# A third load buffer for the tap matrices, one ring for projection inputs and GLU outputs, and another order of the convolution stage

## The chip, the cores and the metric

The kernel runs on one core of one Trainium2 chip. The metric is the device time of one execution in microseconds, as the median of several. A core has TensorE (PE: matrix multiplication, its sums in PSUM banks), VectorE (DVE) and ScalarE (ACT) for work on elements, GpSimd (POOL), which here also issues some transfers, and SyncE (SP), which issues most of them. Each engine takes its instructions in a fixed order and waits for semaphores of the others. Data move between DRAM and the on-chip memory (SBUF, 128 partitions) by DMA engines.

## The reference, cut to what matters

One step of a decoder trunk on 512 prompt tokens and 8 × 8 sample tokens, of width 1024. The stage that is changed is the convolution module of the first layer; the per-layer input `p` of both layers enters far later, but its projection is computed here.

```python
def _conv_module(xn, hist, w_pw1, b_pw1, w_dw, b_dw, ln_g, ln_b, w_pw2, b_pw2):
    u = xn @ w_pw1 + b_pw1
    a, g = jnp.split(u, 2, axis=-1)
    u = a * jax.nn.sigmoid(g)
    ...
    uh = jnp.concatenate([hist.astype(u.dtype), u], axis=1)
    c = _dwconv_valid(uh, w_dw) + b_dw          # 31 taps, each channel by itself
    c = jax.nn.silu(_layernorm(c, ln_g, ln_b))
    return c @ w_pw2 + b_pw2, uh[:, -(CONV_K - 1):]

def _ple(h, p, g, w_gate, w_proj):
    gate = jax.nn.sigmoid(_rmsnorm(h, g) @ w_gate)
    return h + gate * (p @ w_proj)
```

## The kernel before

Each fp32 product is made of three products of rounded parts. A matrix is split into a high part (a cast on ACT, line 172) and a low part (original minus high, on DVE, line 175; for some weights on POOL). TensorE multiplies high by high (184), high by low (186) and low by high (187).

The convolution stage runs from about 50 to 345 us. Tokens are in two parts: part 0 has 256 of the prompt, part 1 the other 256 and the 64 of the samples (320). The 1024 channels are eight blocks m of 128. What happens to a block:

- `pw1(m, part)` (the letter a of the order table): two products into PSUM, `pg` and `pa`, 24 matmuls each; then sigmoid and gate give `u`, a tile in a ring of UB = 3 buffers with the tag "u".
- `d`: `u` is written to DRAM (`d_u`). `regroup(m)` (m in the table) reads it back in another layout into `x`, with 32 channels and 4 pieces of time across the partitions, and splits it into `xx`.
- `taps(m, g)` (c), g = 0 to 3: the prompt's convolution for 32 channels, as 9 pairs of matmuls with a tap matrix. In each pair line 609 multiplies both parts of `xx` by the high part `th`, and line 610 the high part of `xx` by the low part `tl`. There are 32 of these matrices; c(7,3) is the last. `taps_dma(i)` loads matrix i from DRAM into `traw`, on POOL's queue, in a ring of TR = 2 buffers; `taps_load(i)` casts and subtracts it into `th` and `tl`, rings of TB = 2, and then asks for the load of matrix i + TR. Where c(m,g) stands in the table, the split of the next matrix is asked for too. The sums `cps` go out of PSUM as `v` by ACT (613) and DVE (614).
- `ungroup(m)` (b): `v` is written to DRAM (`d_c`, four transfers) and, after that, read back in the first layout into `h` (two transfers), all on SyncE's queue.
- `taps_smp` (o, O): the samples' taps, a product on POOL (636), its sums on DVE.
- `ln_stat(m)` (s): DVE subtracts a mean estimate from block m of `h` (710), ACT squares it (`lsq`, 714), DVE adds the squares up (716), and TensorE forms column sums `lns` (725).

When all eight blocks are in, `ln_y` (L) turns `lns` into factors with a chain of small DVE instructions, and TensorE spreads these over the partitions (`R`). `ln_apply(part)` (M) normalizes and gives `hn`, which the second product `p` (w) takes.

Between these the projection of the per-layer input runs, which depends on none of them: `proj_in(l, part)` (i) loads the input of layer l, `proj_split` (j) splits it into two tiles `pT` with a ring of 4 buffers of their own, and `proj(l, part, half)` (p in the table) is 24 matmuls into four PSUM banks named `proj`. They are copied into `pst` by ACT or DVE (496), a ring of two buffers, and every second copy is followed by a write to DRAM (`d_pp`). All in all there are 192 of these matmuls, 32 copies and 16 writes. `ucat`, in which POOL gathers the last rows of `u` for an output, also has the tag "pst".

The order of each engine's instructions is set by a scheduler from priorities. The priorities follow the order in which the code is emitted, which in this stage is the table `CONV`: one token per step, a letter and its indices, as in

```
a6,0 c3,0 s0 c3,1 o4 j0,0 a6,1 d6 c3,2 O4 c3,3 b3 m5
```

Of the kernel before, what the change touches and what calls it, by code (L numbers as in the profile page):

```python
# [9 lines left out]
F32 = mybir.dt.float32  # L10
F32R = mybir.dt.float32r
# [6 lines left out]
P = 128  # L18
D = 1024
KD = D // P  # L20
# [3 lines left out]
CK = 31  # L24
TAPS = 36
TB = 2
TR = 2
UB = 3
QSB = 5
LBUF = 4  # L30
CONV = """
X0 a0,0 X1 a1,0 a2,0 a0,1 d0 a1,1 d1 o0 m0 a2,1 d2 O0
a3,0 c0,0 m1 c0,1 o1 a3,1 d3 c0,2 O1 c0,3 b0 m2
a4,0 c1,0 c1,1 o2 a4,1 d4 c1,2 O2 c1,3 b1 m3
a5,0 c2,0 k c2,1 o3 a5,1 d5 c2,2 O3 c2,3 b2 m4
a6,0 c3,0 s0 c3,1 o4 j0,0 a6,1 d6 c3,2 O4 c3,3 b3 m5
a7,0 c4,0 s1 c4,1 o5 i0,0 j0,1 c4,2 O5 c4,3 b4 m6 s2
p0,0,0 c5,0 c5,1 o6 i0,1 j1,0 a7,1 d7 c5,2 O6 c5,3 b5 m7 s3
p0,0,1 c6,0 i1,0 j1,1 c6,1 o7 P p0,1,0 c6,2 O7 c6,3 b6 s4
p0,1,1 c7,0 i1,1 c7,1 p1,0,0 c7,2 c7,3 b7 s5  # L40
p1,0,1 s6 s7 L p1,1,0 M0 p1,1,1
w0,0 w1,0 M1 w0,1 w2,0 w1,1 w3,0 n0 w2,1 r0 w3,1 n1 r1
"""
SCHED = """
# [120 lines left out]
class Trunk:  # L165
# [309 lines left out]

    def proj_split(self, l, part, sp):
        n, raw = PN[part], self.praw.pop((l, part))
        pT = [sp.tile([P, 640], F32R, tag="pT", name="pT", bufs=4)[:, :2 * n].rearrange("p (k t) -> p k t", k=2) for _ in range(2)]
        self.hi(pT[0], raw)
        self.lo(pT[1], raw, pT[0])  # L480
        self.pT[l, part] = pT
# [21 lines left out]
    def conv_stage(self):  # L503
# [15 lines left out]
        with tc.tile_pool(name="w2c", bufs=2) as w2, tc.tile_pool(name="cvp", bufs=2) as sp:  # L519
# [13 lines left out]
            def pw1(m, part):  # L533

                n = PN[part]
                if part == 0:
                    us[m] = sp.tile([P, 816], F32, tag="u", name="u", bufs=UB)
                    keep(nc.sync.dma_start(out=us[m][:, 512:], in_=a["sc"][m]))
# [15 lines left out]
                    self.done(("pw1", m, 0), ("pw1", m, 1))  # L554
                    self.V.scalar_tensor_tensor(out=smp(u, 30, 8), in0=pa[:, 256:320].rearrange("p (b t) -> p b t", b=8), scalar=ba, in1=sg[:, 256:320].rearrange("p (b t) -> p b t", b=8), op0=ALU.add, op1=ALU.mult)

            ucat = sp.tile([P, KD, 96], F32, tag="pst", name="ucat")

            def u_out(i):
                keep(nc.gpsimd.tensor_copy(out=ucat[:, i, 0:32].rearrange("p (r q) -> p r q", r=4), in_=us[i][:, 0:512].rearrange("p (r q) -> p r q", r=4)[:, :, 120:128]))  # L560
# [18 lines left out]
            def taps_dma(i):  # L579
                if i < 4 * KD and i not in traw and i not in tw:  # L580
                    traw[i] = sp.tile([P, 32 * TAPS], F32, tag="traw", name="traw", bufs=TR)
                    keep(nc.gpsimd.dma_start(out=traw[i], in_=a["tw"][i]))

            def taps_load(i):
                if i >= 4 * KD or i in tw:
                    return
                taps_dma(i)
                h, l = (sp.tile([P, 32 * TAPS], F32R, tag=n, name=n, bufs=TB) for n in ("th", "tl"))
                raw = traw.pop(i)
                self.hi(h, raw)  # L590
                self.lo(l, raw, h)
                tw[i] = h, l
                taps_dma(i + TR)

            vs = {}

# [19 lines left out]
            def ungroup(m):  # L616

                v = vs.pop(m)
                for r in range(4):
                    nc.sync.dma_start(out=d_c[m][:, :, r].rearrange("g c j -> c g j"), in_=v[32 * r:32 * r + 32])  # L620
                dv = d_c[m].rearrange("g c r j -> (g c) r j")
                for part in PARTS:
                    nc.sync.dma_start(out=cc[part][:, m, 0:256].rearrange("p (r j) -> p r j", r=4), in_=dv[:, :, part * 64:part * 64 + 64])
# [26 lines left out]
            for e in CONV.split():  # L650
                kind, v = e[0], [int(d) for d in e[1:].split(",") if d]
# [14 lines left out]
                    taps(*v)  # L666
                elif kind == "b":
                    ungroup(*v)
                elif kind == "P":
                    dm = self.smp.tile([P, 1], F32, tag="rs_t", name="dm")  # L670
                    self.after(self.A.activation(out=dm, in_=self.zero[:, 0:1], func=AF.Silu), self.sig)
# [714 lines left out]
```

## Time and profile before

| | us |
|---|---|
| median of three runs | 1532.9 |
| lowest and highest of them | 1531.63, 1534.46 |
| the profiled execution | 1532.51 |
| its span | 1530.7 |
| TensorE busy in the span | 1463.4 (96%) |
| VectorE, ScalarE, GpSimd busy | 1041.9, 724.8, 286.6 |
| TensorE busy, 50 to 345 us | 255.60 of 295.00 |
| issue to landing of a tap matrix (576 KB) | 5.1 |

The span is what lies between the first and the last instruction of the profiled execution; its own time has 1.8 us more. The granted clock of TensorE has two levels, shown as 1.00 (2.4 GHz) and 0.50 (1.2 GHz). In a timeline a row is a run of like instructions: start, busy time, engine, line, operation, tiles, count, and in brackets how long the engine was idle before it and what ended this. A row of a wait view gives the waiting engine, tile and line, the releaser, and then total, count and longest.

### The profile page before, as it was taken

What the parts mean: (1) busy time and instruction counts of PE and PEld (TensorE: products, weight loads), DVE (VectorE), ACT (ScalarE), POOL (GpSimd) and SP (SyncE); (2) the same over time, 40 slices, a digit from 0 to 9 for tenths busy, and PEclk for the clock granted to TensorE, in tenths of its full rate; (3) what the DMA queues carried; (4) which work ended last, traced back from release to release, by engine and by line L of the source; (5) the groups of instructions that cost most, each with busy time, mean ns of one, the idle gap of its engine ahead of it and who ended that gap; (6) DMA issues with size and microseconds to landing.
All of it is one profiled execution on the core that took longest, in us unless ns stands there. A gap on an engine that the chain in (4) does not pass through costs nothing.

```text
span 1530.7 us, 27978 instructions
## 1 busy us (share of the span) xinstructions
PE 1463.4 (96%) x10807; PEld 1439.1 (94%) x10807; DVE 1041.9 (68%) x2352; ACT 724.8 (47%) x1580; POOL 286.6 (19%) x430
## 2 busy tenths in 40 slices
PE   8999886899999999999999997999999999999998
PEld 8899776899999999999999996798999999999998
DVE  7687683768655665656877899948765656564774
ACT  5444352635443444444645667744543525252641
POOL 1244440021111211111001333322211111011100
PEclk9999997999999999999999999999999999999999
DMA  5666564433228232323233222214231313131412
GB/s 211 203 203 181 179 215 135 126 122 102 77 76 186 76 103 64 104 66 100 87 115 127 84 70 71 76 52 133 84 97 56 104 49 119 48 122 45 147 46 73
DMA packets 68805, 165.83 MB, mean 108 GB/s; under 512 B 15216, under 2 KB 31056, under 8 KB 68624
## 3 DMA queue, kind: packets, MB, share of 16 engines
q1 hardware_dynamic: 61728, 134.96, 28.7%
q0 software_dynamic: 6640, 28.46, 6.3%
q8 instruction: 85, 1.39, 0.4%
q10 hardware_dynamic: 304, 0.62, 0.1%
q14 instruction: 48, 0.39, 0.1%
HBM read 151.13 MB, written 18.72 MB: 111 GB/s over the span
## 4 chain that ended last, share of the span: by engine, by line
PE 75%; DVE 6%; ACT 2%; issue 1%; DMA 0%; SPq 0%; DVEq 0%; ACTq 0%
PE up L186 12%; PE up L187 12%; PE up L184 12%; PE dn L187 6%; PE dn L186 6%; PE dn L184 6%; PE plg L187 2%; PE plg L186 2%; PE plg L184 2%; PE p L186 1%; PE wo L187 1%; PE wo L184 1%; PE wo L186 1%; PE p L187 1%; PE p L184 1%; DVE qs L175 1%
## 5 line engine op out<-in xcount | busy, mean ns | idle before, releaser
L186 PE MATMUL up<-hn,wh 128*128 128x256 f32 (+1 forms) x1408 | 415.3, 297 | 3.3 <-DVE hn L175 3.3
L187 PE MATMUL up<-hn,wl 128*128 128x256 f32 (+1 forms) x1408 | 413.9, 296 | 0.9 <-DVE wl L175 0.9
L184 PE MATMUL up<-hn,wh 128*128 128x256 f32 (+1 forms) x1408 | 409.8, 296 | 1.0 <-ACT hn L172 1.0
L172 ACT CAST wh<-raw 128x1024 fp32r<-128x1024 f32 x196 | 203.1, 1047 | 307.9 <-PE up L186 173.9
L175 DVE TENSOR_TENSOR wl<-raw,wh 128x1024 fp32r<-128x1024 f32 x173 | 224.0, 1302 | 159.1 <-ACT wh L172 157.3
L186 PEld LDWEIGHTS up<-hn,wh 128*128 128x128 f32 x1408 | 266.1, 189 | 4.1 <-DVE hn L175 3.9
L187 PEld LDWEIGHTS up<-hn,wl 128*128 128x128 f32 x1408 | 266.0, 189 | 1.2 <-DVE wl L175 1.1
L184 PEld LDWEIGHTS up<-hn,wh 128*128 128x128 f32 x1408 | 264.6, 190 | 1.4 <-ACT hn L172 1.4
L187 PE MATMUL dn<-fh,wl 128*128 128x320 f32 (+1 forms) x704 | 208.6, 296 | 0.0
L184 PE MATMUL dn<-fh,wh 128*128 128x320 f32 (+1 forms) x704 | 207.8, 295 | 0.0
L186 PE MATMUL dn<-fl,wh 128*128 128x320 f32 (+1 forms) x704 | 207.7, 295 | 0.0
L797 POOL COPY stash<-ue 128x18 f32<-128x18 f32 x88 | 71.4, 813 | 540.0 <-ACT ue L794 538.4
L827 DVE TENSOR_TENSOR h<-dn,h 128x256 f32<-128x256 f32 (+1 forms) x192 | 87.4, 456 | 98.1 <-PE dn L187 97.9
L184 PEld LDWEIGHTS dn<-fh,wh 128*128 128x128 f32 x704 | 133.6, 190 | 0.0
L187 PEld LDWEIGHTS dn<-fh,wl 128*128 128x128 f32 x704 | 133.0, 189 | 0.0
L186 PEld LDWEIGHTS dn<-fl,wh 128*128 128x128 f32 x704 | 132.9, 189 | 0.0
L609 PE MATMUL cps<-xx,th 128*128 128x256 f32 x288 | 73.8, 343 | 19.1 <-ACT th L172 14.9
L233 POOL TENSOR_TENSOR wl<-raw,wh 128x1024 fp32r<-128x1024 f32 x23 | 55.5, 2425 | 141.8 <-ACT wh L172 130.5
L609 PEld LDWEIGHTS cps<-xx,th 128*128 128x128 f32 x288 | 56.5, 196 | 21.0 <-ACT th L172 16.7
L187 PE MATMUL plg<-hn,wl 128*128 128x256 f32 (+1 forms) x256 | 76.1, 297 | 0.0
L186 PE MATMUL plg<-hn,wh 128*128 128x256 f32 (+1 forms) x256 | 75.9, 297 | 0.0
L184 PE MATMUL plg<-hn,wh 128*128 128x256 f32 (+1 forms) x256 | 75.9, 296 | 0.0
(255 smaller groups left out, 3301.7 us busy)
## 6 DMA issues: line engine op xcount, KB each, us to landing
raw<-in_w_dram SPq DMA_DIRECT2D x196, 512.0 KB, 3.7
traw<-in_tw_dram POOLq DMA_DIRECT2D x32, 576.0 KB, 5.1
bias<-d_bias SPq DMA_DIRECT2D x8, 512.0 KB, 4.5
d_bias<-d_ext POOLq DMA_DIRECT2D x1, 3064.0 KB, 24.8
h<-in_x_dram SPq DMA_DIRECT2D x4, 640.0 KB, 5.4
d_pp<-pst SPq DMA_DIRECT2D x8, 320.0 KB, 3.3
pp<-d_pp SPq DMA_DIRECT2D x8, 320.0 KB, 3.3
d_u<-u SPq DMA_DIRECT2D x8, 256.0 KB, 4.2
```

The lines of the kernel that those rows point to most:

```text
L172: return self.A.copy(out=out, in_=in_)
L175: self.V.tensor_tensor(out=out, in0=in_, in1=hi.bitcast(F32), op=ALU.subtract)
L184: self.after(mm(out, lhsT=wh, rhs=xh, start=start, stop=False), self.hold)
L186: mm(out, lhsT=wh, rhs=xl, start=False, stop=False)
L187: mm(out, lhsT=wl, rhs=xh, start=False, stop=stop)
L233: nc.gpsimd.tensor_tensor(out=l, in0=raw, in1=h.bitcast(F32), op=ALU.subtract)
L609: self.T.matmul(ps[:, 0:2 * P], lhsT=h[:, w], rhs=z[:, :, g, d:d + P], start=d == 0, stop=False)
L797: nc.gpsimd.tensor_copy(out=self.stash[:, :, :, blk], in_=tail)
L827: self.V.tensor_tensor(out=self.h[part][:, m], in0=ps[:, :n], in1=self.h[part][:, m], op=ALU.add)
```

## The change

- The ring of `traw` has three buffers instead of two (TR), and `taps_load(i)` asks for the loads i + 1 to i + TR in order, instead of only i + TR.
- The ring "u" has four buffers instead of three (UB), and `pT` takes its tiles from it. `ucat` has a buffer of its own.
- The transfers `h` of `ungroup` become a step of their own, `bring(m)` (the letter e), which the table has one row later.
- The table is reordered. Before, 144 of the 192 projection matmuls run before the last tap is done and 48 behind `lns`; now 66 run before the last tap is done, 30 between it and `lns`, and 96 behind `lns`. The loads and splits of the projection's inputs (i, j) follow.

```diff
-TR = 2
-UB = 3
+TR = 3
+UB = 4
 ...
-a6,0 c3,0 s0 c3,1 o4 j0,0 a6,1 d6 c3,2 O4 c3,3 b3 m5
+a6,0 c3,0 e2 s0 c3,1 o4 a6,1 d6 c3,2 O4 c3,3 b3 m5
 ...
-p1,0,1 s6 s7 L p1,1,0 M0 p1,1,1
+p0,1,0 p0,1,1 i1,1 s6 s7 L p1,0,0 p1,0,1 M0 p1,1,0 p1,1,1
 ...
-        pT = [sp.tile([P, 640], F32R, tag="pT", name="pT", bufs=4)[:, :2 * n].rearrange("p (k t) -> p k t", k=2) for _ in range(2)]
+        pT = [sp.tile([P, 816], F32R, tag="u", name="pT", bufs=UB)[:, :2 * n].rearrange("p (k t) -> p k t", k=2) for _ in range(2)]
 ...
-            ucat = sp.tile([P, KD, 96], F32, tag="pst", name="ucat")
+            ucat = sp.tile([P, KD, 96], F32, tag="ucat", name="ucat", bufs=1)
 ...
                 tw[i] = h, l
-                taps_dma(i + TR)
+                for k in range(1, TR + 1):
+                    taps_dma(i + k)
 ...
                     nc.sync.dma_start(out=d_c[m][:, :, r].rearrange("g c j -> c g j"), in_=v[32 * r:32 * r + 32])
+
+            def bring(m):
                 dv = d_c[m].rearrange("g c r j -> (g c) r j")
                 for part in PARTS:
                     nc.sync.dma_start(out=cc[part][:, m, 0:256].rearrange("p (r j) -> p r j", r=4), in_=dv[:, :, part * 64:part * 64 + 64])
 ...
+                elif kind == "e":
+                    bring(*v)
```

The first taps. POOL's transfers before (a number tells one tile from another of its name; `DMASW` and `DVE` in brackets are the semaphores that an issue waits for):

```order
L582 DMA traw_795<-in_tw_dram 128x1152
L582 DMA traw_801<-in_tw_dram 128x1152
L582 DMA traw_803<-in_tw_dram 128x1152 [waits DMASW0_49,DVE_49]
L582 DMA traw_809<-in_tw_dram 128x1152 [waits DMASW2_49,DVE_49]
L582 DMA traw_844<-in_tw_dram 128x1152 [waits DMASW1_49,DVE_49]
```

and now:

```order
L582 DMA traw_795<-in_tw_dram 128x1152
L582 DMA traw_801<-in_tw_dram 128x1152
L582 DMA traw_803<-in_tw_dram 128x1152
L582 DMA traw_805<-in_tw_dram 128x1152 [waits DMASW0_49,DVE_49]
L582 DMA traw_811<-in_tw_dram 128x1152 [waits DMASW1_49,DVE_49]
```

The third load no longer waits for a buffer. ACT at the same place, before, where th_805 is the second tap matrix and th_840 the third:

```order
L172 CAST th_797<-traw_795 128x1152 [waits DMASW0_49]
L172 CAST xx_646<-x_171 128x544 [waits DMAHW5_49,DMAHW4_49,DMAHW6_49,DMAHW3_49,Pool_49]
L172 CAST wh_736<-raw_734 128x1024 [waits DMAHW0_49,PE_49]
L548 ACTIVATE sg_790<-sg_790,cols_116 128x256 [waits DVE_49,Activation_49]
L613 ACTIVATE v_830<-cps_811,cols_116 128x128 [waits PE_49]
L172 CAST th_805<-traw_803 128x1152 [waits DMASW2_49]
L172 CAST th_840<-traw_801 128x1152 [waits DMASW1_49,Activation_49]
```

and now, with th_807 the second and th_842 the third:

```order
L172 CAST th_797<-traw_795 128x1152 [waits DMASW0_49]
L172 CAST xx_646<-x_171 128x544 [waits DMAHW5_49,DMAHW4_49,DMAHW6_49,DMAHW3_49,Pool_49]
L172 CAST wh_736<-raw_734 128x1024 [waits DMAHW0_49,PE_49]
L172 CAST th_807<-traw_801 128x1152 [waits DMASW1_49]
L548 ACTIVATE sg_790<-sg_790,cols_116 128x256 [waits DVE_49,Activation_49]
L172 CAST th_842<-traw_803 128x1152 [waits DMASW2_49,PE_49,Activation_49]
L614 ACTIVATE v_832<-cps_813,cols_116 128x128 [waits PE_49]
```

The second matrix is now the one that is loaded second, and its cast has moved ahead of the gate `sg`.

The last taps. ACT before, from the cast of matrix (7,2) to that of (7,3), with `lsq` of block 6 between them:

```order
L172 CAST th_2587<-traw_2477 128x1152
L714 ACTIVATE lsq_2762<-h0_91 128x256
L714 ACTIVATE lsq_2768<-h1_92 128x320
L613 ACTIVATE v_2580<-cps_2591,cols_116 128x128
L496 COPY pst_2631<-proj_2633 128x256
L613 ACTIVATE v_2580<-cps_2664,cols_116 128x128
L496 COPY pst_2649<-proj_2642 128x256
L496 COPY pst_2649<-proj_2651 128x256
L172 CAST th_2660<-traw_2559 128x1152
```

and now, where th_2503 is (7,2) and th_2530 is (7,3):

```order
L496 COPY pst_2460<-proj_2453 128x256
L496 COPY pst_2460<-proj_2462 128x256
L172 CAST th_2503<-traw_2359 128x1152
L614 ACTIVATE v_2494<-cps_2475,cols_116 128x128
L647 ACTIVATE h1_92<-pc_2384,cols_116 128x64
L614 ACTIVATE v_2494<-cps_2507,cols_116 128x128
L172 CAST th_2530<-traw_2395 128x1152
L614 ACTIVATE v_2494<-cps_2534,cols_116 128x128
L719 ACTIVATE lsq_2678<-h0_91 128x256
```

The square of block 6 has moved behind the last cast, and the copies into `pst` that stood ahead of that cast are gone. DVE there, before (tl_2661 is the low part of (7,3), and h0_91 with lnk in the last row is the subtraction of block 7):

```order
L716 TENSOR_TENSOR lss_1635<-lss_1635,lsq_2768 128x320
L614 TENSOR_TENSOR v_2580<-cps_2591,v_2580 128x128
L496 COPY pst_2631<-proj_2612 128x256
L614 TENSOR_TENSOR v_2580<-cps_2664,v_2580 128x128
L175 TENSOR_TENSOR tl_2661<-traw_2559,th_2660 128x1152
L496 COPY pst_2732<-proj_2734 128x256
L614 TENSOR_TENSOR v_2580<-cps_2685,v_2580 128x128
L710 TENSOR_TENSOR h0_91<-h0_91,lnk_1363 128x256
```

and now (tl_2504 is that of (7,2), tl_2531 that of (7,3), h0_91 with lnk is the subtraction of block 6):

```order
L175 TENSOR_TENSOR tl_2504<-traw_2359,th_2503 128x1152
L615 TENSOR_TENSOR v_2494<-cps_2475,v_2494 128x128
L615 TENSOR_TENSOR v_2494<-cps_2507,v_2494 128x128
L715 TENSOR_TENSOR h0_91<-h0_91,lnk_1365 128x256
L175 TENSOR_TENSOR tl_2531<-traw_2395,th_2530 128x1152
L715 TENSOR_TENSOR h1_92<-h1_92,lnk_1369 128x320
L615 TENSOR_TENSOR v_2494<-cps_2534,v_2494 128x128
```

The subtraction of block 6, which stood further ahead, is now between the last two low parts.

The end. TensorE before, from the last two matmuls of c(7,3):

```order
L609 MATMUL cps<-xx,th 128x256
L610 MATMUL cps<-xx,tl 128x128
L725 MATMUL lns<-ones,h_91 128x1 x2
L725 MATMUL lns<-ones,h_92 128x1 x3
L725 MATMUL lns<-ones,h_91 128x1 x2
L725 MATMUL lns<-ones,h_92 128x1 x3
L725 MATMUL lns<-ones,h_91 128x1 x2
L725 MATMUL lns<-ones,h_92 128x1 x3
L725 MATMUL lns<-ones,lss 128x1 x5
L184 MATMUL proj<-pT,wh 128x320
L186 MATMUL proj<-pT,wh 128x320
```

and now, from the last two of the thirty `proj` matmuls that follow c(7,3):

```order
L186 MATMUL proj<-pT,wh 128x320
L187 MATMUL proj<-pT,wl 128x320
L730 MATMUL lns<-ones,h_91 128x1 x2
L730 MATMUL lns<-ones,h_92 128x1 x3
L730 MATMUL lns<-ones,h_91 128x1 x2
L730 MATMUL lns<-ones,h_92 128x1 x3
L730 MATMUL lns<-ones,lss 128x1 x5
L184 MATMUL proj<-pT,wh 128x256
L186 MATMUL proj<-pT,wh 128x256
```

Thirty projection matmuls have moved in between the last tap and the column sums. SyncE's queue there, before (d_c7 and then `h` of the last block):

```order
L498 DMA d_pp10_151<-pst_2732 128x512
L498 DMA d_pp10_151<-pst_2750 128x512
L620 DMA d_c7_188<-v_2580 32x4x128 x4
L623 DMA h0_91<-d_c7_188 128x4x64
L623 DMA h1_92<-d_c7_188 128x4x64
L498 DMA d_pp11_152<-pst_2821 128x640
```

and now:

```order
L498 DMA d_pp01_150<-pst_2608 128x640
L621 DMA d_c7_188<-v_2494 32x4x128 x4
L498 DMA d_pp01_150<-pst_2626 128x640
L498 DMA d_pp01_150<-pst_2644 128x640
L626 DMA h0_91<-d_c7_188 128x4x64
L626 DMA h1_92<-d_c7_188 128x4x64
L473 DMA praw_2599<-in_p1_dram 128x640
```

Two writes of projections have moved in between `d_c7` and the transfers back.

## Rows read from the trace of the kernel before

**Rows 1.** Busy time and granted clock by stretch, whole stage next to last

```profile
core 0: us, PE busy (x) PEld busy (x) DVE busy (x) ACT busy (x) POOL busy (x), PEclk, DMA share, GB/s
68.90:72.30 3.40, 3.40 (x15) 3.40 (x15) 2.97 (x3) 1.28 (x2) 1.28 (x3) 0.50 0.24 55
171.30:178.10 6.80, 5.63 (x27) 5.63 (x27) 5.44 (x9) 3.41 (x7) 2.53 (x2) 0.50 0.37 121
...
243.00:249.80 6.80, 5.49 (x25) 5.49 (x26) 1.78 (x2) 2.00 (x4) 0.00 (x0) 0.50 0.21 77
256.60:270.30 13.70, 10.50 (x43) 10.41 (x44) 5.63 (x26) 1.74 (x4) 0.00 (x0) 0.50 0.15 43
...
50.00:345.00 295.00, 255.60 (x1848) 249.46 (x1847) 206.28 (x346) 127.37 (x219) 84.91 (x70) 0.94 0.56 173
sum 332.50, PE 287.42 PEld 281.20 DVE 228.32 ACT 140.53 POOL 89.46; mean PE 41.06 PEld 40.17 DVE 32.62 ACT 20.08 POOL 12.78
```

**Rows 2.** Waits of TensorE, 62 to 76 us (total, times, longest)

```profile
PE cps L609 <- ACT th L172: 3.4, 1, 3.4
```

**Rows 3.** Waits of TensorE, 166 to 252 us

```profile
PE cps L609 <- ACT th L172: 11.2, 3, 5.1
...
PE cps L609 <- ACT pst L496: 0.8, 1, 0.8
...
PE cps L609 <- DVE pst L496: 0.3, 1, 0.3
```

**Rows 4.** Waits of TensorE, 252 to 300 us

```profile
PE lns L725 <- DVE h L710: 5.7, 2, 5.5
PE p L184 <- ACT hn L172: 2.3, 1, 2.3
PE p L186 <- DVE hn L175: 2.2, 2, 1.2
```

**Rows 5.** Timeline of POOL, 50 to 70 us (start, duration, idle before)

```profile
53.44 1.29 POOL L582 DMA_DIRECT2D traw<-in_tw_dram  x2
61.85 0.53 POOL L582 DMA_DIRECT2D traw<-in_tw_dram  x1 [7.12 <-DVE tl L175]
```

**Rows 6.** Timeline of DVE, 134 to 172 us

```profile
135.88 0.81 DVE L175 TENSOR_TENSOR pT<-praw,pT 128x640 fp32r<-128x640 f32 x1
...
170.50 0.42 DVE L710 TENSOR_TENSOR h<-h,lnk 128x256 f32<-128x256 f32 x1 [4.95 <-DMA h<-d_c]
```

**Rows 7.** Timeline of ACT, 161 to 173 us

```profile
170.96 0.42 ACT L714 ACTIVATE lsq<-h 128x256 f32<-128x256 f32 x1 [6.54 <-DVE h L710]
171.28 1.14 ACT L172 CAST th<-traw 128x1152 fp32r<-128x1152 f32 x1
```

**Rows 8.** Waits of TensorE, 128 to 166 us

```profile
PE cps L610 <- DVE tl L175: 4.4, 4, 1.4
```

**Rows 9.** Waits of ACT, 60 to 262 us

```profile
ACT pst L496 <- DMA d_pp<-pst: 9.9, 4, 4.7
```

**Rows 10.** Timeline of SyncE's queue, 134 to 258 us

```profile
135.35 1.77 SPq L620 DMA_DIRECT2D d_c<-v  x4
...
160.38 1.81 SPq L620 DMA_DIRECT2D d_c<-v  x4
...
166.23 1.20 SPq L623 DMA_DIRECT2D h<-d_c  x2
...
179.49 1.76 SPq L620 DMA_DIRECT2D d_c<-v  x4
...
252.65 1.94 SPq L620 DMA_DIRECT2D d_c<-v  x4
256.53 1.20 SPq L623 DMA_DIRECT2D h<-d_c  x2
```

**Rows 11.** Busy time of the projection's instructions alone, 172 to 252 us

```profile
172.00:252.00 80.00, 24.54 (x144) 22.80 (x144) 2.64 (x6) 6.61 (x18) 0.90 0.64 209
```

**Rows 12.** Timeline of DVE, 251 to 282 us

```profile
276.65 1.22 DVE L175 TENSOR_TENSOR wl<-raw,wh 128x1024 fp32r<-128x1024 f32 x1
```

More of the change, by code (lines that the diff above doesn't have):

```diff
@@ L33 @@
 a3,0 c0,0 m1 c0,1 o1 a3,1 d3 c0,2 O1 c0,3 b0 m2
-a4,0 c1,0 c1,1 o2 a4,1 d4 c1,2 O2 c1,3 b1 m3
-a5,0 c2,0 k c2,1 o3 a5,1 d5 c2,2 O3 c2,3 b2 m4
-a6,0 c3,0 s0 c3,1 o4 j0,0 a6,1 d6 c3,2 O4 c3,3 b3 m5
[L37 to L40, printed above, removed]
-p1,0,1 s6 s7 L p1,1,0 M0 p1,1,1
+a4,0 c1,0 e0 c1,1 o2 a4,1 d4 c1,2 O2 c1,3 b1 m3
+a5,0 c2,0 e1 k c2,1 o3 a5,1 d5 c2,2 O3 c2,3 b2 m4
+a6,0 c3,0 e2 s0 c3,1 o4 a6,1 d6 c3,2 O4 c3,3 b3 m5
+a7,0 c4,0 e3 s1 c4,1 o5 c4,2 O5 c4,3 b4 m6 s2
+c5,0 e4 c5,1 o6 j0,0 a7,1 d7 c5,2 O6 i0,0 c5,3 b5 m7 s3
+p0,0,0 c6,0 e5 c6,1 o7 P j0,1 c6,2 O7 c6,3 b6 s4
+p0,0,1 c7,0 e6 i0,1 c7,1 j1,0 c7,2 s5 i1,0 c7,3 b7 e7 j1,1
+p0,1,0 p0,1,1 i1,1 s6 s7 L p1,0,0 p1,0,1 M0 p1,1,0 p1,1,1
 w0,0 w1,0 M1 w0,1 w2,0 w1,1 w3,0 n0 w2,1 r0 w3,1 n1 r1
```

## The prediction

> **What bounds the kernel now.** I read three views in this order: the busy time and granted clock by stretch, the waits of TensorE by stretch, and then the timelines of the engines that those waits name. The change touches only the convolution stage, from about 50 to 345 us; behind it the order of every engine is the same. In these 295.0 us TensorE is busy for 255.6, so it waits for 39.4 [rows 1]. Six stretches in it run at a granted clock of 0.50, which is 1.2 GHz instead of 2.4. Their busy time is what the sum row has over the row of the whole stage, 287.4 − 255.6 = 31.8 us; at full clock it would have been half of that, so 15.9 us are lost [rows 1]. Waits and clock together, 55 us, are all that an order can win here. The reader should see that a slow stretch follows a long wait: 68.9 follows the wait in [rows 2], 243.0 and 256.6 the longest ones of [rows 3] and [rows 4].
>
> The waits have three causes. First, the second tap matrix is loaded third: POOL issues two loads at 53.44 and the next only at 61.85, after 7.12 us of waiting for DVE to free a buffer [rows 5], and TensorE waits 3.4 us for the cast of that matrix [rows 2]. Second, each block of taps goes through DRAM (`d_c` out, `h` back) and DVE subtracts its mean: that subtraction stands in DVE's queue waiting for the transfer, 4.95 us at 170.50 [rows 6], the square on ACT behind it waits 6.54 us, and the next cast of a tap matrix, 171.28, stands behind the square [rows 7]. Third, after the last tap nothing is left for TensorE until the last block is back: 5.7 us [rows 4].
>
> **First taps.** The three loads now go out in the order in which they are used, with a buffer for each, so the wait of 3.4 goes, and with it the half of 3.40 us at low clock, 1.7 [rows 1, 2]: −5.1. Against it stands a third load of the same size in flight beside the first regrouping of `u`, on which the first tap waits; I allow it between 0 and 2 us, by the 2.0 us that I find below for a transfer beside a tap load, and take 0.5. **−4.6** (−5.1 to −3.1).
>
> **Rows of blocks 2 to 4, up to 166 us.** TensorE waits 4.4 us, four times, for the low part `tl` of a tap matrix [rows 8]. DVE makes it in order; ahead of it stand the split of a projection input, 0.81 us [rows 6] (two of them in these rows), and the subtraction with its wait. The change moves the splits to later rows, and ACT's cast th(3,3) goes ahead of the square of block 2. I leave 1.5 us of the 4.4, one wait of the longest size there. **−2.9** (0, if the subtraction is what delays `tl` everywhere, to −4.4).
>
> **Rows of blocks 4 to 7, 166 to 252 us.** Seven rows of waits, from 11.2 to 0.3 us, come to 18.0 [rows 3], and three slow stretches (the two shown, 5.63 and 5.49, and one of 3.40) to 7.3 of lost clock [rows 1]. Of these go: the two waits for a copy of a projection out of PSUM and one of a projection for `v`, 1.9 us in three (a first of 0.8 and the last of 0.3 are shown [rows 3]), and the mechanism of the longest wait, 5.1: ACT stood there behind copies whose buffer was still being written to DRAM (9.9 us in four waits [rows 9]), and these copies now follow the last tap. Not all of the 5.1 goes. In DVE's order of the changed kernel tl(7,3) stands right behind the subtraction of block 6, and from the issue of `d_c` to that of `h` I count 5.85 and 3.88 us (160.38 to 166.23, 252.65 to 256.53 [rows 10]), before the transfer back has even begun; 3.4 are next late there, so −1.7. What stays: th(4,3) is still behind the square of block 3. What comes: 12 projection matmuls no longer delay TensorE's arrival there, +2.0 by 24.54 us for 144 of them, 0.17 each [rows 11]; and casts th(6,0) and th(7,1) now stand behind the squares of blocks 4 and 5, at 1.0 each, my choice between 0 and 4. −1.9 − 1.7 + 2.0 + 2.0 = 0.4, and 2.4 of the small waits for `tl`, `th` and `v` go with the copies: −2.0. Of the lost clock I take off 2.0, since the longest wait shrinks. **−4** (+6, if the two casts newly behind a square cost 4 each, near the 5.1 of the longest wait, and no slow stretch goes; to −15, if only the wait behind the square of block 3 stays, with one slow stretch).
>
> **The end.** Before: waits of 5.7, 2.3 and 2.2 us [rows 4], and half of 10.50 and of 3.40 us at low clock, 6.9 [rows 1]: 17.1. Now 30 projection matmuls stand between the last tap and the column sums `lns`. At 0.17, or about 0.15 once the stretch from 243.0, 5.49 us in 25 matmuls [rows 1], is counted at full clock, they cover 4.5 of the wait. SyncE has two writes of projections ahead of the last `h` transfer, and DVE one copy ahead of the subtraction; they need 18 of the 30 matmuls, 2.7 us, which is less than the 3.88 that `d_c` needs anyway [rows 10], so they cost nothing unless the clock is low. 2.5 are left of the 5.7 (1.2 to 5.7). Then 48 + 48 projection matmuls, 14 us, lie beside the normalization's chain on DVE. Two splits of weights at 1.22 [rows 12] now stand inside that chain, so its result is some 2 us late for TensorE, a new wait of 2.0 (0 to 3.6). The waits of `p` behind it, 4.5, shrink to 2.0, since TensorE gets there about 5 us later and DVE about 4. Low clock: two stretches of 3.40 instead of 10.50 and 3.40, 3.4. That is 9.9 instead of 17.1. **−7.2** (+1 to −12).
>
> **A rule against this change.** A wait is followed by a slow stretch here, with 1.7 us lost in each of 3.40 us [rows 1]. The Trainium skill, TensorE: Matmul & The Clock Gate, "HAM oscillation — how this bites in real kernels", tells of a loop whose wait for data comes back every turn and drops the clock to 1.2 GHz every time. By that rule, taking the projection out of the rows would add a slow stretch in each of four rows, 6.8 us, and the sum would be 1520 instead of 1513.5. The trace agrees for the long waits alone, since the four waits of [rows 8], of up to 1.4, have no slow stretch behind them among the six; of the forecast's 0.60 below I give this outcome 0.10, the upper edge of its own range.
>
> **The sum.** 1532.5 (the profiled execution) − 4.6 − 2.9 − 4 − 7.2 = 1513.8. The median of the runs shown is 0.4 above the profiled execution, less than the error of any term. I predict 1513.5. A bound on the work: 78 projection matmuls, 11.7 us at 0.15, move behind the last tap, and the end saves 7.2 besides, so the last `d_c`, at 252.65, has to come some 23 us earlier, near 229.5.
>
> **Rivals.** (a) *The third buffer stands idle.* A cast needs one of two `th` buffers, and that frees only with the matmuls two taps before; the load is earlier, the cast is not. The third load also takes part of the transfers: `d_c` to `h` took 5.85 us in the middle of the taps and 3.88 in the last block, when no tap matrix is left to load [rows 10]; 2.0 more in two rows that wait on it is +4, and the gains of the rows go. 1532.5 − 4.6 − 7.2 + 4 = 1525. For it: DVE's wait for `h` in [rows 6]. The Trainium skill, DMA: Bandwidth & Descriptors, "Issuing engines are not separate DMA queues", says that transfers share the same engines whoever issues them, so POOL's loads would slow SyncE's; these two pairs of rows are in line with it, two cases only. Against it: the splits and copies leave the rows in any case. 0.17.
> (b) *Slower.* The rows are paced by the way through DRAM and DVE and not by TensorE. From 135.35 to 160.38 a row took 25.0 us, and the next 19.1 [rows 10]. If each of the four rows after block 3 keeps 25.0, starting 7.5 us earlier, the last `d_c` is issued at 152.9 + 100 = 252.9, no earlier than now, and 11.7 us of projection still come. Less the 7.2 that the end saves (and its 4.5 of cover, counted in that) this is 1532.5 + 0.3 + 11.7 − 7.2 = 1537. It turns slower than before from rows of about 23.8 us. Against it: the four rows took 23.1 each (160.38 to 252.65 [rows 10]) with 18 projection copies of ACT and 6 of DVE in them [rows 11]. 0.09.
> (c) *The rows open.* With copies and splits gone, `h` is back before DVE wants it in every row but that of block 3; of 18.0 + 7.3 us half goes, −12.6 instead of −4: 1505. 0.14.
>
> **How the numbers follow.** Forecast 0.60 (1508 to 1520), (a) 0.17, (b) 0.09, (c) 0.14. The range from 1502 to 1525 leaves out (b), the upper half of (a) and the tail of (c), under 0.2. About 0.2%, 3 us, is what a measurement of this kernel can tell from no change. Faster by more: the forecast, (c) and most of (a), 0.86; within: 0.05, from the tail of (a); slower: 0.09.
>
> **What would show it.** First taps: three loads in one stretch on POOL, no wait of TensorE near 65 us. Rows: waits for `tl` up to 166 us under 2 us; the last `d_c` near 229.5. If it is past 240, (a) or (b) holds, and DVE's waits for `h` say which. End: `lns` waits about 2.5 us, a new wait of `R`, and the stretch of low clock around it shorter than 13.7 us. I am wrong most if the rows, not the loads, set where the last tap ends.

## The result

The changed kernel takes 1513.5 us, the median of four runs (1512.4 to 1517.6), against 1532.3 before: a ratio of 0.9882, 95% interval 0.9859 to 0.9904. A second series gave 1512.5 and 0.9881 (0.9848 to 0.9914). The prediction said 1513.5. The number is right, in part by luck; the reasons behind it are only partly so, and the experiments below show which.

The first profile of the changed kernel caught the longest of its runs, 1517.6. The rows below are from the profile of the second series, whose execution took 1512.1, near the median.

The busy time and the granted clock by stretch of the convolution stage, as in [rows 1]. The four stretches are those at half clock; the row of 50 to 345 us now also holds more of what follows the stage:

```profile
core 0: us, PE busy (x) PEld busy (x) DVE busy (x) ACT busy (x) POOL busy (x), PEclk, DMA share, GB/s
154.20:164.30 10.10, 10.10 (x48) 10.10 (x48) 4.87 (x8) 2.27 (x4) 4.59 (x4) 0.50 0.77 238
188.30:198.50 10.20, 9.74 (x46) 9.45 (x46) 10.20 (x13) 5.95 (x10) 4.46 (x5) 0.50 0.42 160
219.00:232.60 13.60, 12.67 (x56) 12.38 (x54) 6.81 (x13) 3.86 (x8) 0.02 (x1) 0.50 0.48 136
242.90:249.70 6.80, 6.63 (x31) 6.63 (x32) 4.59 (x16) 3.49 (x5) 0.00 (x0) 0.50 0.84 298
50.00:345.00 295.00, 276.96 (x2001) 272.48 (x2000) 227.17 (x392) 136.66 (x247) 86.54 (x72) 0.93 0.56 179
```

All waits of TensorE there (total, times, longest, in us):

```profile
PE cps L611 <- DVE tl L175: 9.8, 7, 2.1
PE lns L730 <- DVE h L715: 2.4, 2, 1.7
PE up L186 <- DVE hn L175: 1.9, 2, 1.6
PE R L285 <- DVE dg L283: 1.3, 1, 1.3
PE cps L610 <- ACT th L172: 1.1, 1, 1.1
PE up L187 <- DVE wl L175: 1.0, 1, 1.0
PE proj L184 <- DVE v L615: 0.5, 1, 0.5
```

The reader should see two things. TensorE waits for 18.0 us instead of 39.4 [rows 1]: the waits for a cast `th`, 11.2 us between 166 and 252 alone [rows 3], are down to 1.1, and those of `p` [rows 4] are gone. But it now spends 39.1 us (the four rows) busy at half clock, where it spent 31.8 before. The waits that are left are all under 2.2 us, and stretches of 10 to 14 us at half clock stand behind three of them in which TensorE hardly waits at all: it is busy for 10.10 of the first 10.10 us.

By the terms of the prediction, waits and half of the busy time at half clock taken together:

| term | before | now | difference | predicted |
|---|---|---|---|---|
| first taps | 5.1 | 0 | −5.1 | −4.6 |
| rows up to 166 us | 4.4 | 2.1 + 5.1 | +2.8 | −2.9 |
| rows from 166 us to the last tap | 18.0 + 7.3 | 9.3 + 11.2 | −4.8 | −4 |
| the end | 10.2 + 6.9 | 3.7 + 3.3 | −10.1 | −7.2 |
| sum | | | −17.2 | −18.7 |

The profiled executions differ by 20.4 us; 3 us lie outside these terms. The last `d_c` is issued at 235.36, between the 229.5 of the forecast and the 240 from which rivals (a) and (b) would have held:

```profile
235.36 1.78 SPq L621 DMA_DIRECT2D d_c<-v  x4
```

(A correction to the part on the kernel before: in the order table `proj_in`, the load, is the letter j and `proj_split` is i.)

### The profile page after: what moved, and what is told of

The parts are those of the page before. It is cut to its first block, busy times and chain, and to the rows that moved or that the text cites. A ratio compares the mean times of both kernels' runs of the same rounds, so it can differ in the third digit from the quotient of the medians.

```text
span 1515.8 us, 27984 instructions
## 1 busy us (share of the span) xinstructions
PE 1468.7 (97%) x10807; PEld 1446.3 (95%) x10807; DVE 1043.2 (69%) x2352; ACT 723.5 (48%) x1580; POOL 288.7 (19%) x430
## 4 chain that ended last, share of the span: by engine, by line
PE 81%; DVE 9%; DMA 4%; issue 2%; ACT 2%; SPq 1%; POOL 1%; DVEq 0%; POOLq 0%; ACTq 0%
PE up L186 12%; PE up L187 12%; PE up L184 12%; PE dn L187 6%; PE dn L186 6%; PE dn L184 6%; PE plg L187 2%; PE plg L186 2%; PE plg L184 2%; PE cps L610 2%; DMA d_c<-v 2%; DVE wl L175 1%; DMA h<-d_c 1%; DVE tl L175 1%; PE p L186 1%
## 5 line engine op out<-in xcount | busy, mean ns | idle before, releaser
L610 PE MATMUL cps<-xx,th 128*128 128x256 f32 x288 | 80.0, 368 | 4.8 <-ACT th L172 3.2
L611 PE MATMUL cps<-xx,tl 128*128 128x128 f32 x288 | 69.8, 242 | 6.9 <-DVE tl L175 6.9
```

The source lines that it names most:

```text
L610: self.T.matmul(ps[:, 0:2 * P], lhsT=h[:, w], rhs=z[:, :, g, d:d + P], start=d == 0, stop=False)
L611: self.T.matmul(ps[:, 0:P], lhsT=l[:, w], rhs=z[:, 0, g, d:d + P], start=False, stop=d == nd - 1)
```

## Experiments

All of these kernels compute the whole reference. Each ratio is to the kernel before, timed beside it.

### The same kernel again: is the low clock chance?

> The changed kernel as it is, once more. What is asked is its clock. In the first profile the waits of TensorE from 50 to 345 us fell from 39.3 to 20.9 us, but the time at half clock rose, from 31.8 us busy at half clock to 44; the stretches stand at 156, 170, 201, 221 and 245 us, where taps and the one-column matmuls lns run alone. Theory 1 (the order makes them: the rows have lost the projection that kept the clock up): the same stretches at the same places, 35 to 48 us busy at half clock, and a time of 1512 to 1515. Rival (chance): the stretches move or are gone in this profile, with under 30 us in all and a time that follows them.

Measured: 1512.5, ratio 0.9881 (0.9848 to 0.9914). Busy at half clock: 39.1 us in this profile and 44 in the first. The stretches stand at 154, 188, 219 and 243 us, in the first profile at 156, 170, 201, 221 and 245. Those at 155, 220 and 244 recur; the one at 170 doesn't, and the one at about 190 to 200 moves. This fits theory 1 for most of it: the low clock comes with this order, with some chance in where it begins. These are two profiles only.

### The order of the loads alone

```diff
-                taps_dma(i + TR)
+                for k in range(1, TR + 1):
+                    taps_dma(i + k)
```

on the kernel before, with TR = 2.

> The kernel before, with the loads of tap matrices asked for in order (the loop over i + 1 to i + TR) and two buffers still. Theory 1 (the wait at 65 us comes from the order of the loads, and two buffers do): the wait of 3.4 us and the slow stretch of 3.4 us behind it go, 1.5 us may come back at the first taps: 1527 to 1530. Rival (it takes the third buffer): the time stays at 1532.

Measured: 1528.0, ratio 0.9980 (0.9961 to 0.9998), −3.0 us. TensorE no longer waits at 65 us. So the first taps don't need the third buffer, as theory 1 said; asking in order does it. Some 3.0 of the 4.6 us are there, by an interval that reaches from 0.3 to 6.

### Everything but the order, and the order alone

The first is the changed kernel with the old table, each e directly behind its b. The second is the kernel before with the new table, without e:

```diff
-CONV = (the old table)
+CONV = (the new table, without e)
 TR = 2
 UB = 3
```

> The changed kernel with the old order table, the transfers back directly behind the writes as before: three buffers, requests in order and the shared ring remain. Theory 1: the first taps alone, -4.6 us, and nothing in the rows, since a cast waits for one of two th buffers: 1526 to 1529. Rival (the third buffer does more, by earlier casts in the rows): below 1522.

> The kernel before with the new order table alone: two buffers for loads, the old request rule, pT in a ring of its own, the transfers back directly behind the writes. Theory 1: the end gains 7 to 10 us and the rows little, and the wait of the first taps stays: 1517 to 1522. Rival (the order needs the third buffer and the later transfers back): 1526 or more. If it reaches 1514, the buffers do nothing beside it.

Measured: everything but the order 1517.4, ratio 0.9907 (0.9877 to 0.9938); the order alone 1536.3, ratio 1.0036 (1.0018 to 1.0055). Both theories of mine fall. The buffers and the request rule bring some 14 us without the new order, and with the new order alone the kernel is 5 us slower. On top of the buffers the order gains some 4 to 5, and there the two intervals overlap. Waits of TensorE in the order alone, 50 to 345 us, and two rows of ACT's timeline in it (start, duration, idle before, releaser):

```profile
PE cps L610 <- DVE tl L175: 14.4, 9, 4.3
PE cps L609 <- ACT th L172: 14.0, 4, 7.7
```

```profile
236.92 0.62 ACT L172 CAST pT<-praw 128x512 fp32r<-128x512 f32 x1 [5.56 <-DMA praw<-in_p_dram]
237.44 2.20 ACT L172 CAST th<-traw 128x1152 fp32r<-128x1152 f32 x2
```

Here the longest wait, 7.7 us, is for a cast that stands on ACT behind the split of a projection input, and this split waits 5.56 us for its load. So moving the projection put a new waiting instruction ahead of tap work.

By its profile this is not what makes the kernel slower than the one before. The first matmul behind the stage, in the kernel before and then in this one:

```profile
334.81 0.52 PE L184 MATMUL up<-hn,wh 128*128 128x256 f32 x3
```

```profile
329.47 0.52 PE L184 MATMUL up<-hn,wh 128*128 128x256 f32 x3
```

The new order alone ends the stage 5.3 us earlier, and yet this execution takes 5.4 us longer in all. What it loses lies behind the stage, in a part that the change leaves as it was. Some of it is seen in the clock: from 900 to 1080 us the granted clock is 0.91 on average, and 0.96 in the same part of the kernel before (905 to 1085). Why is open, and so is whether every execution does this.

### Which of the buffers

Three kernels: the ring alone on the kernel before (UB = 4, `pT` in it, `ucat` apart); three load buffers and requests in order on the kernel before, with `pT` in the ring of three to make room; and the changed kernel with TR = 2.

> The kernel before with the shared ring alone: UB = 4, pT in the ring of u, ucat with a buffer of its own; old order, two load buffers, old request rule. Theory 2 (third load buffer): 1528 or more. Rival (shared ring): 1522 or less. In this kernel's order 6 of the 48 projection matmuls behind c(7,2) come behind the last tap.

> The kernel before with three load buffers and requests in order; pT goes into the ring of u to make room, but this ring stays at three. Old order. Theory 2 (third load buffer): 1521 or less, as the old order with everything gave 1517.4, with 24 projection matmuls behind the last tap as there. Rival (the ring of four is needed): 1527 or more.

> The changed kernel with two load buffers instead of three; the order table, the shared ring of four and the requests in order stay. Known by now: old order with all the rest of the change 1517.4, new order with none of it 1536.3, both 1512.5, neither 1531.0. Theory 2 (the third load buffer carries most of what the rest brings, since casts no longer wait for loads): 1522 or more. Rival (the shared ring of four does, by where it lets the projection's splits go): 1516 or less.

Measured: 1524.4, ratio 0.9941 (0.9923 to 0.9958); 1526.2, ratio 0.9968 (0.9952 to 0.9983); 1529.4, ratio 0.9977 (0.9960 to 0.9995). In the old order the kernel with the ring gains 9 us and the one with the loads 5, and these add up to the 14 that both bring; neither "2" nor its rival is right there. Neither is one edit alone. Of the 5, the order of the requests brings 3.0 by itself, and `pT` stands in a smaller ring there. The kernel with the ring also gives `ucat` a buffer of its own, and in its trace ACT waits 0.3 us from 60 to 262 us for a `pst` to be written out, where it waited 9.9 before [rows 9]; which of its edits brings the 9 us was not tried.

In the new order the third load buffer is worth 15 us, as theory 2 said. With two buffers TensorE's waits for casts are back, and so is what causes them. Waits of TensorE with two buffers, 50 to 345 us:

```profile
PE cps L610 <- ACT th L172: 17.2, 5, 6.9
PE cps L611 <- DVE tl L175: 9.0, 10, 1.7
```

ACT's timeline there, where the casts of (6,3) and (7,2) stand behind squares:

```profile
218.15 0.42 ACT L719 ACTIVATE lsq<-h 128x256 f32<-128x256 f32 x1 [5.21 <-DVE h L715]
218.75 0.47 ACT L719 ACTIVATE lsq<-h 128x320 f32<-128x320 f32 x1 [0.18 <-DVE h L715]
219.12 1.13 ACT L172 CAST th<-traw 128x1152 fp32r<-128x1152 f32 x1
...
238.62 0.42 ACT L719 ACTIVATE lsq<-h 128x256 f32<-128x256 f32 x1 [4.95 <-DVE h L715]
238.94 1.14 ACT L172 CAST th<-traw 128x1152 fp32r<-128x1152 f32 x1
```

The casts wait for nothing but the instruction ahead of them: no bracket stands behind them, while the squares were idle for 5.21 and 4.95 us. The matrices landed at 213.5 and 234.2. With the third buffer the order is another. The squares are those of blocks 5 and 6, and both casts stand ahead of them in the changed kernel; its ACT, from the cast (6,3) and the square of block 5 to the cast (7,2) and the square of block 6:

```profile
202.94 1.15 ACT L172 CAST th<-traw 128x1152 fp32r<-128x1152 f32 x1 [0.61 <-PE cps L610]
...
209.97 0.42 ACT L719 ACTIVATE lsq<-h 128x256 f32<-128x256 f32 x1 [2.61 <-DVE h L715]
...
217.14 1.17 ACT L172 CAST th<-traw 128x1152 fp32r<-128x1152 f32 x1
...
227.87 0.42 ACT L719 ACTIVATE lsq<-h 128x256 f32<-128x256 f32 x1 [1.95 <-DVE h L715]
```

### Two buffers, with the order that three bring

The changed kernel with TR = 2, and with a rule that orders the subtraction and the square of a block behind the last tap work emitted so far. It adds no wait on a semaphore, only an order on the same engine. `last_th` and `last_tl` are the cast and the low part that the table asked for last (the lines that keep them are left out):

```diff
-            self.V.tensor_tensor(out=x, in0=x, in1=self.lnk[part][:, :n], op=ALU.subtract)
+            self.after(self.V.tensor_tensor(out=x, in0=x, in1=self.lnk[part][:, :n], op=ALU.subtract), self.last_tl)
 ...
-            self.A.activation(out=t[:, :n], in_=x, func=AF.Square)
+            self.after(self.A.activation(out=t[:, :n], in_=x, func=AF.Square), self.last_th)
```

> The changed kernel with two load buffers, and with the subtraction and the square of a block ordered behind the last tap cast and low part that the table has emitted by then (a rule for the order of ACT and DVE, no new wait). Known: with three buffers 1512.5, with two 1529.4. In the profile with two, the casts (4,3), (6,3) and (7,2) stand behind a square on ACT and TensorE waits 4.8, 3.4 and 6.9 us for them; with three they stand ahead of it. Theory 3 (the third buffer acts through the order: a load that comes earlier lets the scheduler put the cast ahead of the square): 1520 or less, no wait for th over 2 us. Rival (the loads themselves are late with two buffers): 1526 or more, the same waits ended by loads.

Measured: 1512.2, ratio 0.9871 (0.9845 to 0.9897), the time of the changed kernel with one buffer less. TensorE's waits for casts:

```profile
PE cps L611 <- DVE tl L175: 9.6, 6, 3.1
PE cps L610 <- ACT th L172: 1.6, 2, 0.9
```

17.2 us have become 1.6, as theory 3 said. (One of the three casts that I named, (4,3), stands behind the square with three buffers too. That square waits 6.62 us there and 6.59 with two; TensorE waits 1.1 us for the cast with three and 4.8 with two.) Some casts do wait for their own load here, one of them 4.04 us, but TensorE waits no more than 0.9 us for any cast. So an order alone, with two buffers, brings what the third buffer brought without it. Why the scheduler gives another order with three is not shown; it places instructions by a simulated timeline (`schedule_with_timeline_sim` in the kernel), and a load that is there earlier in it would let the cast go ahead of a square that waits.

### Three buffers and the same rule

> The changed kernel (three load buffers) with the same rule of order for the subtraction and the square. Known: 1512.5 without the rule; its waits for tl of 2.1, 2.0, 1.4 and 1.9 us stand behind a subtraction that waits for the transfer h (5 to 6 us of DVE). Theory 3 (what is left in the rows is the subtraction and the square ahead of tap work): these waits go, 1503 to 1509. Rival (the work only comes later, in a lump behind the last tap, and the end grows by as much): 1511 to 1516.

Measured: 1507.9, ratio 0.9849 (0.9828 to 0.9870), inside the expectation of theory 3, and faster than both kernels. With the kernels of the sections before, this makes a table:

| | two load buffers | three |
|---|---|---|
| without the rule | 1529.4 (0.9977) | 1512.5 (0.9881) |
| with the rule | 1512.2 (0.9871) | 1507.9 (0.9849) |

The third buffer is worth 15 us by the ratios without the rule, and 3 with it, where the intervals overlap. So most of what it brings is the order; whether something is left that it does as a buffer is open.

The number is that of theory 3, the reason only in part. Of the four waits that I named, only that of 2.0 us stands behind a subtraction that waits for `h` (4.89 us). And TensorE waits more in this kernel, 22.0 us from 50 to 345 us instead of 18.0. What shrinks is the time at half clock, from 39.1 us busy to 21.3 in four stretches, which is worth 8.9 us. The first two stretches, and the sum of the four:

```profile
158.90:162.20 3.30, 3.30 (x18) 3.30 (x17) 2.70 (x5) 0.80 (x1) 0.57 (x2) 0.50 0.54 179
186.20:189.50 3.30, 3.30 (x17) 3.30 (x17) 1.69 (x4) 1.54 (x4) 0.44 (x1) 0.50 0.77 214
...
sum 30.10, PE 21.30 PEld 21.02 DVE 16.09 ACT 10.22 POOL 1.01; mean PE 5.32 PEld 5.26 DVE 4.02 ACT 2.55 POOL 0.25
```

These two stand behind waits of 2.20 and 2.07 us and are over after 3.3 us. In the changed kernel waits of 2.10 and 2.05 us have stretches of 10 us behind them. A group of the one-column matmuls `lns` stands in each of those, and none in these two; the rule puts the subtraction later, and with it the column sums. That the columns make the difference is not shown by this (see the last experiment).

The waits for `tl` fall from 9.8 to 4.7 us, and one long wait comes up, 7.4 us for the last cast:

```profile
PE cps L610 <- ACT th L172: 8.5, 2, 7.4
PE cps L611 <- DVE tl L175: 4.7, 3, 2.2
```

On ACT, and on SyncE's queue ahead of it:

```profile
216.62 0.62 ACT L172 CAST pT<-praw 128x512 fp32r<-128x512 f32 x1 [7.65 <-DMA praw<-in_p_dram]
217.15 0.36 ACT L614 ACTIVATE v<-cps,cols 128x128 f32<-128x128 f32 x1
217.41 1.14 ACT L172 CAST th<-traw 128x1152 fp32r<-128x1152 f32 x1
```

```profile
205.31 0.40 SPq L498 DMA_DIRECT2D d_pp<-pst  x1
212.47 1.20 SPq L626 DMA_DIRECT2D h<-d_c  x2
213.72 0.62 SPq L473 DMA_DIRECT2D praw<-in_p_dram  x1
```

It is the same pattern a third time: the load of a projection input stands on SyncE behind `h`, which waits for `d_c`; its split waits 7.65 us on ACT; and the cast of the last tap matrix stands behind it, although nothing needs that split before the last tap.

### And the split behind the last cast

On top of that kernel:

```diff
-        self.hi(pT[0], raw)
+        self.after(self.hi(pT[0], raw), self.last_th)
 ...
-p0,0,1 c7,0 e6 i0,1 c7,1 j1,0 c7,2 s5 i1,0 c7,3 b7 e7 j1,1
+p0,0,1 c7,0 e6 i0,1 c7,1 j1,0 c7,2 s5 c7,3 b7 e7 i1,0 j1,1
```

> The kernel force (changed kernel, subtraction and square ordered behind the last tap work emitted; 1507.9), with the high part of a projection input ordered behind the last cast in the same way, and the split of part (1,0) emitted behind the last tap. In the profile of force the longest wait left in the rows is 7.4 us for th(7,3); ACT stands there in the split of this input, which waits 7.65 us for its load behind the transfers h on SyncE's queue. Theory 3 (one waiting instruction ahead of a cast sets the row): the wait goes, with 6.2 us busy at half clock beside it: 1498 to 1503. Rival (the load of matrix (7,3), which landed at 212, or the subtraction of block 6 is next late there at nearly the same time): 1506 to 1509.

Measured: 1501.8, ratio 0.9825 (0.9791 to 0.9859): inside theory 3 again, and the fastest kernel here, some 9 to 12 us below the changed one. The step from 1507.9 is not clear of the noise, as the intervals of the two ratios overlap and the four runs go from 1498.6 to 1509.6. TensorE's waits fall from 22.0 to 14.7 us, and the wait of 7.4 is gone. ACT at the same place:

```profile
210.02 1.14 ACT L172 CAST th<-traw 128x1152 fp32r<-128x1152 f32 x1
213.41 0.62 ACT L172 CAST pT<-praw 128x512 fp32r<-128x512 f32 x1 [2.25 <-DMA praw<-in_p_dram]
```

The split still waits, but nothing of the taps stands behind it.

### The cover behind the last tap

The changed kernel with all of the second half of the projection behind `lns`:

```diff
-p0,1,0 p0,1,1 i1,1 s6 s7 L p1,0,0 p1,0,1 M0 p1,1,0 p1,1,1
+i1,1 s6 s7 p0,1,0 p0,1,1 L p1,0,0 p1,0,1 M0 p1,1,0 p1,1,1
```

> The changed kernel with the 30 projection matmuls between the last tap and the column sums put behind these (144 behind lns, and none between). Theory 1 (the cover is worth what it fills): TensorE's waits for lns grow from 2.4 to 6 or 7 us and the low clock there lasts one or two stretches of 3.4 longer; the same matmuls lie beside the normalization chain instead, where TensorE waits 1.3 us for R: 1515 to 1519. Rival (the place does not matter, as the chain behind hides them as well): 1511 to 1514.

Measured: 1523.9, ratio 0.9945 (0.9927 to 0.9963). The place of these 30 is worth some 10 us, more than the 3 to 6 expected. The wait for `lns` grows from 2.4 to 5.5 us (6 or 7 expected), but two other things come with it:

```profile
226.60:250.40 23.80, 16.44 (x70) 16.27 (x71) 9.65 (x34) 3.52 (x8) 0.00 (x0) 0.50 0.34 109
```

```profile
PE lns L730 <- DVE h L715: 5.5, 2, 5.0
PE proj L184 <- ACT pst L496: 2.8, 1, 2.8
```

The clock stays at half for 23.8 us on end, and the 144 projection matmuls in a row run into their own output: TensorE waits 2.8 us for a bank whose copy on ACT waits 4.78 us for one of the two `pst` buffers to be written out. In the terms of the end: 3.1 us for `lns`, 2.8 for the bank, 4.9 for the clock (half of 16.44 against half of 6.63), less 1.3 as the wait for `R` is gone, together 9.5. So of the 10 us only some 3 are the wait that the cover fills. Another 18 matmuls went with the 30, out of the taps before c(7,3) is done.

### Are the column sums what keeps the clock low?

The changed kernel with all `lns` columns formed behind the last tap, block by block as before, in one loop at s7.

> The changed kernel with the column sums lns of all blocks formed behind the last tap instead of block by block in the rows: the same matmuls, later. In the profile of the changed kernel each of the stretches at half clock in the rows has one group of these one-column matmuls in it (10 records, 2.2 us at half clock). Theory 4 (these groups keep the clock low): at most 25 us busy at half clock from 50 to 345 us instead of 39 to 44, and 1506 to 1511. Rival (the clock falls for the waits, and the columns only happen to stand there; the columns are now on the path behind the last tap): the stretches stay, 1512 to 1518.

Measured: 1523.2, ratio 0.9935 (0.9909 to 0.9960), slower than both expectations. Theory 4 falls as it was put: with no column sums in the rows, stretches at half clock stand there still, and with the one behind the last tap they have 38.4 us busy.

```profile
161.80:171.90 10.10, 5.00 (x24) 5.00 (x24) 5.72 (x9) 3.38 (x6) 2.03 (x2) 0.50 0.32 89
189.10:195.80 6.70, 4.88 (x23) 4.59 (x23) 6.70 (x8) 2.51 (x5) 4.14 (x4) 0.50 0.37 133
216.40:223.10 6.70, 6.70 (x32) 6.70 (x33) 3.17 (x6) 0.60 (x2) 0.00 (x0) 0.50 0.63 175
226.60:233.30 6.70, 4.95 (x19) 4.95 (x20) 3.04 (x4) 2.12 (x4) 0.00 (x0) 0.50 0.01 2
243.70:260.60 16.90, 16.90 (x80) 16.90 (x80) 8.45 (x29) 4.34 (x7) 0.00 (x0) 0.50 0.61 213
```

In the rows the low clock stands at waits, of which this kernel has longer ones (up to 6.7 us for `tl`). But the rival, that the clock falls for the waits alone, does not hold either. The last stretch has no wait near it. TensorE's last one ends at 228.35; then come taps and projection, and from 239.91 the column sums of all blocks without a break:

```profile
239.91 13.67 PE L732 MATMUL lns<-ones,h 128*128 128x1 f32 x80
```

Ten more follow, to 255.57. TensorE is busy the whole time, the granted clock is 1.00 until 243 us and 0.50 from 243.70, inside this run, and it is back at 1.00 after 260.60, when projection matmuls have run for 5 us. So a run of one-column matmuls can stand before a fall of the clock without any wait. As the waits in the rows are longer in this kernel, it doesn't show what the columns do there; what sets how long a stretch lasts stays open.

## Why the prediction was right, and where it was wrong

**The sum** was right to a tenth of a per cent, and this is luck, by errors that cancel: 5.7 us too much for the rows up to 166 us against 2.9 too little for the end, 0.5 for the first taps, 0.8 for the later rows, and some 3 us outside the terms.

**First taps: right in size, wrong in part in its cause.** I gave each load a buffer of its own as the reason. The order of the requests alone takes the wait away with two buffers, and brings 3.0 us. The three loads now go out in one run on POOL, as I said they would:

```profile
55.94 1.82 POOL L582 DMA_DIRECT2D traw<-in_tw_dram  x3
```

**Rows up to 166 us: wrong.** The waits for `tl` fell about as forecast, from 4.4 to 2.1. The step that failed is that I took the low clock there as unchanged. Behind a wait of 2.1 us stands a stretch at half clock of 10.1 us, 5.1 us lost. "The trace agrees for the long waits alone" was the mistake: in the rows of before the four short waits had no stretch behind them, and I took this as a rule. By the Trainium skill, TensorE: Matmul & The Clock Gate, "HAM oscillation — how this bites in real kernels", I had priced a slow stretch in each of four rows, 6.8 us, as an outcome of 0.10. Three came, longer than 3.4 us each, and over the rows they take 16.3 us where 7.3 was lost before. Here the page's warning was nearer than my reading, though the loop that it tells of waits longer each turn than the 1.9 to 2.1 us before these stretches. It was outweighed because the waits went down by more than I thought.

**Rows from 166 us on: right in size by luck, wrong in cause.** This is the term that matters. I forecast 2.0 us less waiting and 2.0 less at the clock; measured are 8.7 less waiting and 3.9 more at the clock. I put the gain down to copies and splits that leave the rows, and held the third buffer to be worth nothing there: "a cast needs one of two `th` buffers" stood behind rival (a). The runs show otherwise. The kernel with the order alone is 5 us slower than the one before, and the changed kernel without the third buffer loses 15 us. In that kernel the casts that cost most did not wait for a `th` buffer; they stood behind a square. I had read this in [rows 7], and had seen in the two orders that the square of block 6 moved behind the last cast. The step I didn't take was to ask why it moved. With two buffers a rule of order brings the same time as the third buffer does, so most of its worth is the order. The +2.0 for casts newly behind squares did not come: TensorE waits 1.1 us for a cast in all, and that is (4,3).

**The end: right in kind, 2.9 us too small.** The `lns` waits are 2.4 (2.5 forecast), the new wait for `R` is 1.3 (2.0), and the low clock 6.63 us busy (two stretches of 3.40). The mis-sized term is the waits of `p`: 4.5 before, 2.0 forecast, none measured. The 30 matmuls of the cover are not what takes these away, since the kernel without the cover has none either; with the old order and all the rest they are 4.5 still. So they go with the 96 or more matmuls behind `lns`. What the cover fills is seen in the wait for `lns`, 5.5 us without it and 2.4 with it.

**Rival (b), slower,** has no support as a mechanism. The new order by itself is slower, by 0.36%, but its stage ends earlier than that of the kernel before. It is not the way through DRAM alone that paces the rows; a rule of order brings some 16 us with two buffers and the same transfers. One waiting instruction ahead of a cast does it, a square in one kernel and the split of an input in another.

**Not settled:** the transfers back as a step of their own were never tried alone. The kernel with everything but the order, and the one with the order alone, both have them directly behind the writes. Nor were the parts of the 9 us of the ring taken apart.

## What to carry to other kernels

When an engine's row shows a long idle and the instruction behind it is the one that others wait for, ask first what stands ahead of it, not whether its data came late: an instruction without a bracket of its own, behind one with 5 us, is late by order alone, if its own data had landed. A buffer can change the order that a scheduler chooses, and an explicit rule of order may do the same without the memory; here it gave 1512.2 with two buffers and 1507.9 with three, and 1501.8 with the split ordered too. Add up waits and time at half clock separately before naming a cause: the rule with three buffers won by the clock while the waits grew. Take a change of buffers and order apart in both directions before crediting either, since one alone may lose what both together gain.

## What the runs showed of the hardware

Short waits can cost clock too. Behind waits of 2.1, 2.0 and 1.9 us in the changed kernel the granted clock was at half for 10 to 14 us while TensorE was busy for 93 to 100% of the time; behind waits of 2.20 and 2.07 us in the kernel with the rule of order it was so for 3.3 us. In the kernel with all column sums late it fell inside a run of one-column matmuls, with no wait for 15 us. The clock, not the waits, is the larger half of what the changed kernel loses in the stage: 19.6 of 37.6 us.

A subtraction on DVE of 1.36 us took 4.49 beside a product on POOL, and TensorE's wait of 1.4 us at 208.66 stands behind it. The waits of 2.1 and 1.9 us stand behind other DVE instructions that POOL's products stretch in the same way, a low part of a weight from 1.21 to 3.05 us and a subtraction of the mean from 0.48 to 3.10. DVE's and POOL's timelines in the changed kernel:

```profile
202.09 1.36 DVE L175 TENSOR_TENSOR tl<-traw,th 128x1152 fp32r<-128x1152 f32 x1 [1.69 <-ACT th L172]
...
204.12 4.49 DVE L175 TENSOR_TENSOR tl<-traw,th 128x1152 fp32r<-128x1152 f32 x1 [0.47 <-ACT th L172]
```

```profile
204.29 3.10 POOL L639 TENSOR_TENSOR pr<-u,cols 128x1024 f32<-128x1024 f32 x1
```

4.49 is 1.36 and the 3.10 of POOL's product. The Trainium skill, SBUF — State Buffer, "SBUF: two separate sides", says that a VectorE instruction with two inputs from SBUF and a GpSimd instruction that reads SBUF hold a common port in turn, each for its whole length; the lengths in these rows agree, to 0.03 us. Which of the two had the port first they don't show: DVE's row begins 0.17 us before POOL's.
